# Transposing a retention head's normalised rows by DMA, as two planes of 16-bit halves, in place of TensorE

## The chip, the core and the metric

The kernel runs on one core of a Trainium2 chip. A core has five engines that each work through their own list of instructions in order: TensorE (PE, matmuls; its weight loads are PEld), VectorE (DVE), ScalarE (ACT), GpSimd (POOL) and SyncE (SP), which here issues all the DMAs. [...] On-chip data lie in SBUF, 128 partitions; a matmul writes into one of the banks of PSUM, which the other engines then read. DMAs move data between HBM and SBUF, and between places of SBUF. The metric is the device time of one execution in microseconds; lower is better.

## The reference

One layer of a hybrid decoder trunk on 2048 rows of width 1024, with 16 learned rows put ahead of them. What matters here, in the reference's words:

```python
hn = rms_norm(h, norm_g)
proj = jnp.einsum('bld,de->ble', hn, w_in)
cx, cb, cc, cg, q, k, v, rg = jnp.split(proj, N_PROJ, axis=-1)
conv_out = short_conv_branch(cx, cb, cc, conv_w) * jax.nn.silu(cg)
qf = rotary(q, pos) * d ** -0.5;  kf = rotary(k, pos)
ret = head_group_norm(retention_chunkwise(qf, kf, vf), ret_norm_g)
ret_out = ret.astype(h.dtype) * jax.nn.silu(rg)
mixed = jnp.concatenate([conv_out, ret_out], axis=-1)
h = h + jnp.einsum('ble,ed->bld', mixed, w_out)      # then a final rms_norm
```

There are four retention heads of 128 columns and four groups of 128 columns of the convolution. The retention of a head works on chunks of 128 rows. `head_group_norm` takes mean and variance over a head's 128 columns in each row, and the result is multiplied by a gain and by silu of the gate `rg`. The layer is in float32.

## The kernel before

**Stages.** The 2048 rows are worked in two stages of 1024 (`r` = 0, 1), each of two halves of 512 (`j` = 0, 1), and after them comes the output projection in eight pairs of row blocks. A stage has eight units: four convolution groups and four retention heads. Stage one runs group 0 first, then heads 0 to 3, then the other groups; stage two heads 0 to 3, then the groups (`UNITS`, line 36).

**A unit** has two quads. A quad (lines 203 to 238) makes a 2 by 2 arrangement of 128 by 512 blocks of the input projection by Strassen's scheme, in Winograd's form: seven products, each of 12 matmuls of 512 columns (four slices of the inner dimension, each as three matmuls on values split into a high part and a remainder). The products accumulate in three PSUM banks: xb, yb and zb. The tag of these banks, `pj`, has four, taken in rotation, so product 1 of a quad (its yb) goes into the bank that held yb of the quad before. ScalarE copies some of the banks out (`tc`, line 219) and VectorE adds (`take`). A bank can be written again once its `take` has read it: for the first quad of a head the `take` of yb is the addition that makes the first kv tile (line 587, at the helper's line 110).

**Weights.** `stationary` (line 123) takes four loaded blocks (`ra`, line 436 issues the loads), makes three combinations on GpSimd, and splits each of the seven into `wh` (ScalarE's cast, line 101) and `wl` (VectorE's subtraction, line 113), in rings of three.

**A head's tail.** After its second quad, the head (line 575) transposes k and v, makes the states, and for each half `j` the scores (`sc`, line 659), the masked scores (`pm`, line 661) and the output `o` (lines 669 and 670, eight short matmuls into one bank). Then it normalises: statistics on VectorE (lines 675 and 677), the root on GpSimd (`rp`, line 682), the normalised rows `y` on VectorE (line 686). Four transposes on TensorE (line 693) into a bank `yT` put rows and columns the way the gate lies, and VectorE multiplies by gain and gate (line 694); `store_mixed` sends the half out (line 444).

**What sets the order.** The program is written unit by unit, but a scheduler of the framework puts each engine's instructions into an order by its own estimate of their times; so a head's tail is worked in among the matmuls of the next unit's first quad. The order is fixed when the program is built. DMAs wait on SyncE in their order: a DMA that waits holds back those behind it.

**Beside the heads** a generator prepares the combinations of the next operand: after heads 1 and 2 of stage one, eight loads of x (line 361), four to each step, are scaled on ScalarE (line 177), combined on VectorE (`block_sums`, line 174 and line 113) and stored (line 190). After heads 1 and 2 of stage two the same is done with w_out, without the scaling. General tiles (`gen`, line 92) come from one pool of 16, taken in rotation: x, kv, q, the gates, and others.

Of the kernel before, what the change touches and what calls it, by code (L numbers as in the profile page):

```python
# [8 lines left out]
F32 = mybir.dt.float32  # L9
F32R = mybir.dt.float32r  # L10
BF16 = mybir.dt.bfloat16
AF = mybir.ActivationFunctionType
ALU = mybir.AluOpType

P = 128
# [6 lines left out]
HB = 512  # L22
# [48 lines left out]
def hybrid_trunk(ctx: ExitStack, tc: tile.TileContext, t, out: bass.AP, chunk_decay):  # L71
# [51 lines left out]
    def stationary(blocks):  # L123

        a11, a12, a21, a22 = blocks
        s1 = sb.tile([P, HB], F32, name="sa", tag="ra", bufs=RAW)

        def parts(src):
            hi = sb.tile([P, HB], F32R, name="wh", tag="wh", bufs=RING)
            lo = sb.tile([P, HB], F32R, name="wl", tag="wl", bufs=RING)  # L130
            split(hi, lo, src)
            return hi, lo

        w = [parts(a11), parts(a12)]
        add(nc.gpsimd, s1, a21, a22)
        sub(nc.gpsimd, a21, a11, a21)
        sub(nc.gpsimd, a11, s1, a11)
        sub(nc.gpsimd, a12, a12, a11)
        return w + [parts(a) for a in (a11, s1, a21, a12, a22)]
# [53 lines left out]
    def prepared(m, src, ns, held={}):  # L193

        for n in ns:
            for kt in range(KH):
# [3 lines left out]
                    nc.sync.dma_start(a, src[n, kt])  # L200
                parts(m, SUMS[n], kt, a)

    def quad(w, m, take):


        def product(i, bank, first):
            (wh, wl) = w[i]
            for kt in range(KH):
                ks = slice(kt * P, (kt + 1) * P)
                mh, ml = m[i][kt]  # L210
                for n, (a, b) in enumerate(((wl, mh), (wh, ml), (wh, mh))):
                    nc.tensor.matmul(  # L212
                        bank, a[:, ks], b, start=first and kt == 0 and n == 0, stop=kt == KH - 1 and n == 2,
                        skip_group_check=not first,
                    )

        def copy(bank):
            c = sb.tile([P, HB], F32, name="tc", tag="tc", bufs=COPIES)
            nc.scalar.copy(out=c, in_=bank)  # L219
            return c  # L220

        xb = ps_proj()
        product(0, xb, True)
        c = copy(xb)
        yb = ps_proj()
        product(1, yb, True)
        take(0, 0, yb, c)
        product(2, xb, False)
        u2 = copy(xb)
        zb = ps_proj()  # L230
        product(3, zb, True)
        c = copy(zb)
        product(4, xb, False)
        take(1, 1, xb, c)
        product(5, zb, False)
        take(0, 1, zb, u2)
        product(6, xb, False)
        take(1, 0, xb, None)
# [276 lines left out]
    def conv_group(g, r, m, f, blocks, ahead):  # L515
# [20 lines left out]

        blocks, meta = blocks
        quad(stationary(blocks), m, take)
        if meta:
            meta_carry(g, meta)  # L540
        carry(u, g, r)
# [24 lines left out]
    def rotary(a, table):  # L566
# [5 lines left out]
        nc.vector.tensor_tensor(out=a, in0=a, in1=table[:, 0, :], op=ALU.mult)  # L572
        turned[0] = nc.vector.tensor_tensor(out=a, in0=a, in1=rot[:, :w], op=ALU.add)

    def head(h, r, m, rot_t, f, blocks, ahead, first=(), between=()):


# [16 lines left out]
        if len(first) > 0:  # L594
            quad_plain(first[0], m, take)
        else:
            quad(stationary(blocks[0]), m, take)
        next(between, lambda: None)()
        q, sg = [None, None], [None, None]

# [54 lines left out]
        for j in range(2):  # L655
# [28 lines left out]
            for c in range(CH):  # L684
# [2 lines left out]
                    out=y[:, cs], in0=o[:, cs], scalar1=mv[:, c, 0:1], scalar2=rp[:, c, :],  # L687
                    op0=ALU.subtract, op1=ALU.mult,
                )
            yT = ps_misc()  # L690
            for c in range(CH):
                cs = slice(c * P, (c + 1) * P)
                nc.tensor.transpose(yT[:, cs], y[:, cs], ident)  # L693
            nc.vector.scalar_tensor_tensor(
                out=sg[j], in0=yT, scalar=ret_g[:, h : h + 1], in1=sg[j], op0=ALU.mult, op1=ALU.mult
            )
            store_mixed(r, j, KH + h, sg[j])
        if r < NR - 1:
            nc.gpsimd.tensor_copy(out=state[h], in_=states[-1])
        return blocks  # L700
# [203 lines left out]
```

## Time and profile before

| | |
|---|---|
| median of 3 runs | 894.16 us (893.94 to 894.59) |
| the profiled execution | 893.76 us |
| its span | 892.0 us |
| TensorE busy | 879.8 us, 99% of the span |
| VectorE busy | 717.7 us, 80% |
| ScalarE busy | 407.2 us, 46% |
| GpSimd busy | 397.8 us, 45% |
| moved by DMA | 116.94 MB, 131 GB/s on the mean |
| transposes of y on TensorE | 64, in 16 groups of four |

The span is the time from the first to the last record of the profile; the execution's own time is 1.8 us longer. In the profile a line such as L212 is line 212 of the kernel; the instructions of a helper (`add`, line 110; `sub`, line 113; the cast of `split`, line 101) all have the helper's line, so they are told apart by their tiles: `wl<-ra,wh` is a weight's remainder, `kv<-pj,tc` a kv tile taken from a bank. `128x512` is partitions by elements. What a matmul record shows as its duration (390 ns and more) overlaps the next; the distance between starts is its pace. In the changed kernel the lines are later by 3 (up to line 538), by 4 (to line 573) and then by 33 to 35, so L212 becomes L215, L669 and L670 become L704 and L705, and L686 becomes L721.

### The profile page before, as it was taken

Reading aid. Unit: us, or ns where it says so; the run is one execution under the profiler, and the core shown is the slowest. Engines: PE = TensorE matmul, PEld = TensorE weight load, DVE = VectorE, ACT = ScalarE, POOL = GpSimd, SP = SyncE. Lnnn points to the kernel's source line nnn. Section 1 sums busy time; section 2 is a strip of 40 time slices with the busy share of each in tenths; the row PEclk is TensorE's granted clock in tenths of the full one; section 3 lists DMA queues with packets and bytes.
Section 4 is the critical chain, followed back from the end, with each engine's and each line's share of the span. In section 5 each row is a group of like instructions: output and inputs, shape, how many; then the busy total and the mean of one; then the engine's idle time right before and its main releaser. Section 6 shows DMA issues by size and latency. Waiting matters only on the chain.

```text
span 892.0 us, 12867 instructions
## 1 busy us (share of the span) xinstructions
PE 879.8 (99%) x4407; PEld 725.0 (81%) x4407; DVE 717.7 (80%) x1176; ACT 407.2 (46%) x816; POOL 397.8 (45%) x291
## 2 busy tenths in 40 slices
PE   8999999999999999999999999999999999999996
PEld 5778788888888778888888888888888888788885
DVE  6788887988967966999889899777668699766764
ACT  8674424234245364746243332423333476545553
POOL 0554222313134654452323323345546454787773
PEclk9999999999999999999999999999999999999999
DMA  9711224354224252834135272313131393555532
GB/s 336 231 65 48 72 54 150 129 159 149 73 83 142 83 154 75 293 117 141 48 95 200 71 245 87 96 58 95 49 93 49 117 390 101 183 165 160 183 121 81
DMA packets 76242, 116.94 MB, mean 131 GB/s; under 512 B 7632, under 2 KB 24336, under 8 KB 76176
## 3 DMA queue, kind: packets, MB, share of 16 engines
q1 hardware_dynamic: 76176, 116.11, 40.3%
q8 instruction: 35, 0.57, 0.3%
q14 instruction: 31, 0.25, 0.1%
HBM read 90.92 MB, written 25.17 MB: 130 GB/s over the span
## 4 chain that ended last, share of the span: by engine, by line
PE 82%; DVE 8%; DMA 4%; issue 2%; ACT 2%; POOL 2%; SPq 0%; POOLq 0%; DVEq 0%; ACTq 0%
PE pj L212 66%; PE pj L262 6%; DVE ml L113 2%; PE ms L669 1%; PE ms L670 1%; PE ms L659 1%; PE ms L646 1%; DMA w<-in_w_out 1%; DMA ra<-in_w_in 1%; PE ms L397 1%; DVE wl L113 1%; PE ms L693 1%; DVE ml L105 1%; PE ms L631 1%; PE ms L636 1%
## 5 line engine op out<-in xcount | busy, mean ns | idle before, releaser
L212 PE MATMUL pj<-mh,wl 128*128 128x512 f32 x1008 | 399.1, 396 | 1.5 <-ACT wh L101 0.6
L212 PE MATMUL pj<-ml,wh 128*128 128x512 f32 x1008 | 393.3, 390 | 0.0
L212 PE MATMUL pj<-mh,wh 128*128 128x512 f32 x1008 | 393.0, 390 | 0.0
L101 ACT CAST wh<-ra 128x512 fp32r<-128x512 f32 x216 | 134.0, 621 | 311.0 <-PE pj L212 264.9
L212 PEld LDWEIGHTS pj<-mh,wl 128*128 128x128 f32 x1008 | 189.4, 188 | 43.2 <-issue 2.2
L113 DVE TENSOR_TENSOR wl<-ra,wh 128x512 fp32r<-128x512 f32 x216 | 194.1, 899 | 34.5 <-ACT wh L101 34.0
L212 PEld LDWEIGHTS pj<-mh,wh 128*128 128x128 f32 x1008 | 189.2, 188 | 39.9
L212 PEld LDWEIGHTS pj<-ml,wh 128*128 128x128 f32 x1008 | 189.5, 188 | 37.8 <-issue 0.5
L113 POOL TENSOR_TENSOR ra<-ra 128x512 f32<-128x512 f32 x72 | 112.8, 1566 | 84.1 <-DVE qg L614 32.3
L110 POOL TENSOR_TENSOR sa<-ra 128x512 f32<-128x512 f32 x36 | 54.9, 1526 | 120.6 <-DVE wl L113 53.1
L113 POOL TENSOR_TENSOR ra<-sa,ra 128x512 f32<-128x512 f32 x36 | 52.0, 1444 | 92.6 <-DVE wl L113 89.1
L219 ACT COPY tc<-pj 128x512 f32<-128x512 f32 x108 | 62.7, 580 | 0.0
L262 PE MATMUL pj<-ml,mh 128*128 128x512 f32 x128 | 50.2, 392 | 0.1
L262 PE MATMUL pj<-mh,mh 128*128 128x512 f32 x128 | 49.9, 392 | 0.0
L262 PE MATMUL pj<-mh,ml 128*128 128x512 f32 x128 | 48.7, 397 | 0.7 <-DVE ml L113 0.6
L682 POOL TENSOR_TENSOR rp<-rs,neg_half 128x4 f32<-128x4 f32 x16 | 19.9, 1246 | 48.1 <-DVE rs L110 47.8
L723 DVE TENSOR_TENSOR yo<-pj,yo 128x512 f32<-128x512 f32 x32 | 21.9, 686 | 17.6 <-PE pj L212 7.8
L101 ACT CAST wh<-sa 128x512 fp32r<-128x512 f32 x36 | 22.4, 621 | 29.1 <-PE pj L212 28.9
L522 POOL TENSOR_TENSOR c<-c,rr 128x512 f32<-128x512 f32 x14 | 26.1, 1865 | 19.6 <-DVE c L459 9.6
L686 DVE TENSOR_SCALAR pm<-ms,mv,rp 128x128 f32<-128x128 f32 x64 | 21.9, 404 | 15.8 <-POOL rp L682 15.8
L522 POOL TENSOR_TENSOR c<-c,tc 128x512 f32<-128x512 f32 x14 | 26.1, 1862 | 18.7 <-ACT tc L548 18.7
L728 POOL TENSOR_TENSOR z<-yo,final_g 128x512 f32<-128x512 f32 x16 | 26.9, 1682 | 15.9 <-DVE yo L723 15.9
(137 smaller groups left out, 1145.5 us busy)
## 6 DMA issues: line engine op xcount, KB each, us to landing
ra<-in_w_in SPq DMA_DIRECT2D x128, 256.0 KB, 2.7
x<-in_xT SPq DMA_DIRECT2D x48, 256.0 KB, 4.8
w<-in_w_out SPq DMA_DIRECT2D x32, 256.0 KB, 5.2
ra<-mixed SPq DMA_DIRECT2D x32, 256.0 KB, 2.6
yo<-in_x SPq DMA_DIRECT2D x32, 256.0 KB, 4.5
ra<-in_x SPq DMA_DIRECT2D x16, 256.0 KB, 3.2
mixed<-c SPq DMA_DIRECT2D x16, 256.0 KB, 2.6
mixed<-qg SPq DMA_DIRECT2D x16, 256.0 KB, 2.3
```

Source lines behind the costliest of these rows:

```text
L101: nc.scalar.copy(out=hi, in_=src)
L105: nc.vector.scalar_tensor_tensor(out=lo, in0=src, scalar=scale, in1=hi.bitcast(F32), op0=ALU.mult, op1=ALU.subtract)
L110: eng.tensor_tensor(out=out, in0=a, in1=b, op=ALU.add)
L113: eng.tensor_tensor(out=out, in0=a, in1=b, op=ALU.subtract)
L212: nc.tensor.matmul(bank, a[:, ks], b, start=first and kt == 0 and n == 0, stop=kt == KH - 1 and n == 2, skip_group_check=not first,)
L219: nc.scalar.copy(out=c, in_=bank)
L262: nc.tensor.matmul(banks[i], a[:, ks], b, start=half + kt + n == 0, stop=half == 1 and kt == KH - 1 and n == 2,)
L522: eng.tensor_tensor(out=out, in0=a, in1=b, op=ALU.mult)
L682: nc.gpsimd.tensor_tensor(out=rp, in0=rs, in1=neg_half.rearrange("p (c a) -> p c a", a=1), op=ALU.pow)
L686: nc.vector.tensor_scalar(out=y[:, cs], in0=o[:, cs], scalar1=mv[:, c, 0:1], scalar2=rp[:, c, :], op0=ALU.subtract, op1=ALU.mult,)
L723: last[0] = nc.vector.tensor_tensor(out=y, in0=pp, in1=y, op=ALU.add)
L728: nc.gpsimd.tensor_tensor(out=ys[i][j], in0=y, in1=final_g[:, j * HB : (j + 1) * HB], op=ALU.mult)
```

## The change

A head no longer transposes `y` on TensorE. ScalarE copies `y` into a tile `pl` so that the low 16 bits of all its 512 values stand in one plane and the high 16 bits in another. One DMA with transposing, issued by SyncE, takes `pl` as eight blocks of 128 by 128 16-bit values and writes the transposed blocks into a tile `tr`. A second copy of ScalarE puts the two planes together again, into a tile `wo`. VectorE's multiplication by gain and gate then reads `wo` in SBUF in place of a PSUM bank. The copy back, the gating and the store of both halves are put on a list (`pending`) and are written into the program only after the next unit's first quad (`catch_up`); an edge keeps ScalarE's part of them behind the quad's last copy out of a bank. The three new tiles come from the pool of 16 general tiles, whose size stays.

```diff
+    copied = [None]
...
-            nc.scalar.copy(out=c, in_=bank)
+            copied[0] = nc.scalar.copy(out=c, in_=bank)
...
         quad(stationary(blocks), m, take)
+        catch_up()
...
+    def halves(a):
+        return a.bitcast(U16).rearrange("p (n two) -> p two n", two=2)
+
+    def planes(a):
+        return a.bitcast(U16).rearrange("p (two n) -> p two n", two=2)
+
+    def turn(a):
+        apart, across = gen("pl")[:, :HB], gen("tr")[:, :HB]
+        nc.scalar.copy(out=planes(apart), in_=halves(a))
+        nc.sync.dma_start(
+            across.bitcast(U16).rearrange("p (c f) -> p c f", c=2 * CH), apart.bitcast(U16), transpose=True
+        )
+        return across
+
+    def whole(across):
+        a = gen("wo")[:, :HB]
+        nc.scalar.copy(out=halves(a), in_=planes(across))
+        return a
+
+    pending = []
+
+    def catch_up():
+        if pending:
+            with tc.issue_after(copied[0].ins):
+                while pending:
+                    pending.pop(0)()
...
             quad(stationary(blocks[0]), m, take)
+            catch_up()
...
-            yT = ps_misc()
-            for c in range(CH):
-                cs = slice(c * P, (c + 1) * P)
-                nc.tensor.transpose(yT[:, cs], y[:, cs], ident)
-            nc.vector.scalar_tensor_tensor(
-                out=sg[j], in0=yT, scalar=ret_g[:, h : h + 1], in1=sg[j], op0=ALU.mult, op1=ALU.mult
-            )
-            store_mixed(r, j, KH + h, sg[j])
+
+            def finish(j=j, across=turn(y)):
+                nc.vector.scalar_tensor_tensor(
+                    out=sg[j], in0=whole(across), scalar=ret_g[:, h : h + 1], in1=sg[j], op0=ALU.mult, op1=ALU.mult
+                )
+                store_mixed(r, j, KH + h, sg[j])
+
+            pending.append(finish)
```

The change moves instructions on every engine around a head's tail. Three places follow. Numbers behind a name tell buffers of one name apart, `x4` at a row's end is four equal rows.

**First place: VectorE in stage one, from head 0's tail to head 1.** Before, around the first half's normalisation (`st_1168` to `pm_1157`; `kv_1296`, the first kv tile of head 1, stands 16 rows further up):

```order
L113 TENSOR_TENSOR wl_1265<-ra_1070,wh_1264 128x512
L110 TENSOR_TENSOR kv_1344<-pj_1268,tc_1330 128x512
L113 TENSOR_TENSOR wl_1389<-ra_1379,wh_1388 128x512
L675 BN_STATS st_1168<-ms_1159 128x6 x4
L677 BN_AGGR mv_1169<-st_1168 128x2 x4
L110 TENSOR_TENSOR rs_1178<-mv_1169,ev_402 128x4
L686 TENSOR_SCALAR pm_1157<-ms_1159,mv_1169,rp_1180 128x128 x4
L110 TENSOR_TENSOR kv_1358<-pj_1317,tc_1315 128x512
```

Now, around the second half's normalisation (`st_1206` to `pm_1195`):

```order
L114 TENSOR_TENSOR wl_1403<-ra_1381,wh_1402 128x512
L710 BN_STATS st_1206<-ms_1197 128x6 x4
L712 BN_AGGR mv_1207<-st_1206 128x2 x4
L111 TENSOR_TENSOR rs_1216<-mv_1207,ev_442 128x4
L721 TENSOR_SCALAR pm_1195<-ms_1197,mv_1207,rp_1218 128x128 x4
L111 TENSOR_TENSOR kv_1290<-pj_1277,tc_1275 128x512
L111 TENSOR_TENSOR kv_1338<-pj_1262,tc_1324 128x512
L111 TENSOR_TENSOR kv_1352<-pj_1311,tc_1309 128x512
```

Before, two of the three additions that free banks (`kv_1296`, `kv_1344`) stood ahead of the head's normalisation; now all three stand behind the normalisation of both halves.

TensorE at this place now (`ms_1197` is the output of the second half, `pj_1422` product 0 of head 1's second quad and `pj_1437` its product 1, which takes the bank of `pj_1277`):

```order
L215 MATMUL pj_1422<-mh03_145,wh_1390 128x512
L704 MATMUL ms_1197<-kv_838,pm_1195 128x128
L705 MATMUL ms_1197<-state_1121,qg_1025 128x128
L704 MATMUL ms_1197<-kv_838,pm_1195 128x128
L705 MATMUL ms_1197<-state_1144,qg_1025 128x128
L704 MATMUL ms_1197<-kv_838,pm_1195 128x128
L705 MATMUL ms_1197<-state_1146,qg_1025 128x128
L704 MATMUL ms_1197<-kv_838,pm_1195 128x128
L705 MATMUL ms_1197<-state_1148,qg_1025 128x128
L215 MATMUL pj_1437<-mh10_163,wl_1395 128x512
```

Before, products 5 and 6 of the first quad and most of product 0 of the second stood behind the first half's eight short matmuls, and the second half's came one product later, behind product 1. Now product 1 follows the second half's directly.

**Second place: stage one, from head 1's tail to head 2** (and the same from 2 to 3). SyncE before (`mixed` are the stores of a finished half, `x` the loads and `sums_x` the stores of the preparation):

```order
L415 DMA mr<-in_rot_m 16x256
L436 DMA ra<-in_w_in 128x512
L444 DMA mixed_89<-qg 128x4x128
L361 DMA x<-in_xT 128x512 x8
L190 DMA sums_x<-x 128x512
L436 DMA ra<-in_w_in 128x512
L190 DMA sums_x<-x 128x512 x4
```

and now:

```order
L439 DMA ra<-in_w_in 128x512 x6
L590 DMA_TRANSPOSE tr<-pl 128x8x128
L439 DMA ra<-in_w_in 128x512
L590 DMA_TRANSPOSE tr<-pl 128x8x128
L364 DMA x<-in_xT 128x512 x8
L191 DMA sums_x<-x 128x512 x8
L447 DMA mixed_88<-qg 128x4x128
```

VectorE there now (`pm_1678` is the second half's normalised rows, `x_1714` a step of the preparation, `kv_1807` the first kv tile of head 2):

```order
L710 BN_STATS st_1689<-ms_1680 128x6 x4
L712 BN_AGGR mv_1690<-st_1689 128x2 x4
L111 TENSOR_TENSOR rs_1699<-mv_1690,ev_442 128x4
L721 TENSOR_SCALAR pm_1678<-ms_1680,mv_1690,rp_1701 128x128 x4
L175 SCALAR_TENSOR_TENSOR x_1714<-x_1714,gain_69,x_1712 128x512
L111 TENSOR_TENSOR kv_1807<-pj_1794,tc_1792 128x512
L111 TENSOR_TENSOR kv_1855<-pj_1779,tc_1841 128x512
```

The x loads stood behind the store of a finished half and now stand behind both transposing DMAs; a step that uses two of them now stands between the normalisation and the first kv addition. On TensorE the order there is that of the first place.

**Third place: stage two, from head 1's tail to head 2** (and from 2 to 3), VectorE now (`w_4877` and `w_4875` are two loads of w_out, issued behind both transposing DMAs):

```order
L710 BN_STATS st_4853<-ms_4844 128x6 x4
L712 BN_AGGR mv_4854<-st_4853 128x2 x4
L111 TENSOR_TENSOR rs_4863<-mv_4854,ev_3797 128x4
L721 TENSOR_SCALAR pm_4842<-ms_4844,mv_4854,rp_4865 128x128 x4
L114 TENSOR_TENSOR wl_5073<-ra_5061,wh_5072 128x512
L114 TENSOR_TENSOR wl_5081<-ra_5059,wh_5080 128x512
L114 TENSOR_TENSOR w_4877<-w_4877,w_4875 128x512
L111 TENSOR_TENSOR kv_4968<-pj_4955,tc_4953 128x512
```

Here too the first kv addition stands behind the second half's normalisation and behind a step of the preparation. On TensorE three products (the last of the old first quad but one, product 0 and product 2 of the next quad) stand between that half's short matmuls and product 1, which needs the bank.

More of the change, by code (lines that the diff above doesn't have):

```diff
@@ L11 @@
 BF16 = mybir.dt.bfloat16
+U16 = mybir.dt.uint16
 AF = mybir.ActivationFunctionType
```

## The prediction

> **What bounds the kernel now.** I read the page first, then the chain of waits, then TensorE's waits, then the timeline at the tail of a head. The page's busy shares, slices and chain:
>
> ```profile
> PE 879.8 (99%) x4407; PEld 725.0 (81%) x4407; DVE 717.7 (80%) x1176; ACT 407.2 (46%) x816; POOL 397.8 (45%) x291
> PE   8999999999999999999999999999999999999996
> PEclk9999999999999999999999999999999999999999
> PE 82%; DVE 8%; DMA 4%; issue 2%; ACT 2%; POOL 2%; SPq 0%; POOLq 0%; DVEq 0%; ACTq 0%
> ```
>
> TensorE is busy in every slice at the full granted clock, and 82% of the chain is its own. A busy TensorE need not be at its peak, so the pace counts. Two pieces of the chain in order of time (start, us, what), then three rows of TensorE's waits (us in total, times, longest):
>
> ```profile
> 118.63 7.50 PE pj L212 x33
> 767.63 117.31 PE pj L212 x516
> ...
> PE pj L212 <- ACT wh L101: 0.6, 1, 0.6
> PE pj L212 <- ACT tc L219: 0.5, 1, 0.5
> PE ms L693 <- DVE pm L686: 0.3, 1, 0.3
> ```
>
> Both pieces go at 0.227 us a 512-column matmul (7.50/33, 117.31/516), and hardly any matmul waits. So whatever leaves TensorE is won in full, and whatever makes it wait is lost in full. The order of its instructions is fixed, so a lost wait is not made up later.
>
> **What is removed: 64 transposes.** All of L693, and one group of four in the timeline (start, duration):
>
> ```profile
> L693 PEld LDWEIGHTS ms<-ident,pm x64: 138/140/146, 125.7 to 605.9; 128*128 128x128 f32 x64
> L693 PE MATMUL ms<-ident,pm x64: 270/272/329, 126.0 to 606.1; 128*128 128x128 f32 x64
> ...
> 140.48 0.39 PE L212 MATMUL pj<-mh,wh 128*128 128x512 f32 x1
> 140.72 0.60 PE L693 MATMUL ms<-ident,pm 128*128 128x128 f32 x4
> 141.07 0.48 PE L212 MATMUL pj<-mh,wl 128*128 128x512 f32 x1
> 141.38 0.40 PE L212 MATMUL pj<-ml,wh 128*128 128x512 f32 x1
> ```
>
> The 270 ns overlap. From 140.48 to 141.38 pass 0.90 us, in which two plain matmuls would take 0.45; the four transposes cost 0.45, handover included. 16 groups: **-7.1 us**. Below that only 6 us or so could be meant, where a group stands among other short matmuls; more than 7.1 is not there.
>
> **What hides.** 32 ScalarE copies of 1024 halves are added. A 512-column copy and the smallest instruction beside it:
>
> ```profile
> L101 ACT CAST wh<-ra 128x512 fp32r<-128x512 f32 x216 | 134.0, 621 | 311.0 <-PE pj L212 264.9
> L321 ACT ACTIVATION_READ_ACCUMULATOR n<-n x16: 185/187/192, 281.4 to 332.6; 128x1 f32 x16
> ```
>
> 0.62 for 512 and 0.19 for one element give about 1.06 us for 1024 (estimate; no less than 0.62, no more than 1.24). 34 us in all are covered by ScalarE's 311 us of idling ahead of these casts, 265 of it for TensorE; without that cover they would cost up to 34. The gating on VectorE keeps its count and reads SBUF in place of PSUM: nothing. 16 transfers of 256 KB are 4 MB beside 117: nothing by volume.
>
> **What is moved: a chain of VectorE now stands ahead of a bank that TensorE needs.** In the order of the changed kernel the last eight short matmuls of a head (its second half's output, L704 and L705) stand directly ahead of product 1 of the next quad. That product writes the bank of product 1 of the quad before, which VectorE frees with the addition of the first kv tile. Ahead of this addition VectorE now has the second half's whole normalisation, which needs those same short matmuls. So TensorE stands still from the end of them until statistics, square root, normalisation and addition are through. In the kernel before, 33 matmuls of 512 columns stood between the first half's output and the first matmul that needs anything behind its chain. The same chain, once, in the timeline of before (TensorE's first matmul behind the short ones, then VectorE, with GpSimd's root):
>
> ```profile
> 118.39 0.48 PE L212 MATMUL pj<-mh,wl 128*128 128x512 f32 x1
> ...
> 118.67 0.89 DVE L675 BATCH_NORM_STATS2 st<-ms 128x6 f32<-128x128 f32 x4 [0.43 <-PE ms L670]
> 119.48 0.36 DVE L677 BATCH_NORM_AGGREGATE mv<-st 128x2 f32<-128x6 f32 x4
> 119.87 0.17 DVE L110 TENSOR_TENSOR rs<-mv,ev 128x4 f32<-128x4 f32 x1
> 121.17 1.37 DVE L686 TENSOR_SCALAR pm<-ms,mv,rp 128x128 f32<-128x128 f32 x4 [1.13 <-POOL rp L682]
> 122.46 0.68 DVE L110 TENSOR_TENSOR kv<-pj,tc 128x512 f32<-128x512 f32 x1
> ...
> 120.12 1.02 POOL L682 TENSOR_TENSOR rp<-rs,neg_half 128x4 f32<-128x4 f32 x1
> ```
>
> Counted from 118.39, when TensorE could go on, normalisation ends at +4.15 and the addition at +4.75. **First stage, head 0 to head 1: +4.75 us.** Less only if the additions were ahead of the chain, which the order excludes.
>
> **First stage, heads 1 to 2 and 2 to 3: more.** There the order puts one step of preparing x (L175) between the chain and the addition. It needs x loads which SyncE issues only behind the second transposing DMA, and that DMA waits for ScalarE's copy of the normalised rows. The eight x loads of before, in a window of their own, and one such step of VectorE:
>
> ```profile
> L361 SPq DMA_DIRECT2D x<-in_xT x8: 382/400/457, 142.8 to 146.2; - x8
> ...
> DMA to landing us min/median/max: 3.0/4.0/4.7
> ...
> 154.44 0.74 DVE L174 SCALAR_TENSOR_TENSOR x<-x,gain 128x512 f32<-128x512 f32 x1
> ```
>
> From the same zero: 4.15 (normalised), +1.06 (copy into planes), + issue of the transposing DMA, + the second x load, + 0.74 + 0.68. The second load is issued 0.5 after the first and lands between 3.0 and 4.0 later, say 4.1 from the first issue. The issue is not in the trace: a plain one takes 0.40, eight of them (the instruction names eight blocks of 128 by 128) 3.2; I take 1.6, since it is one instruction with more to describe than a plain one, nearer to the lower row. Its 256 KB on the same queue delay the loads behind it: the first x load lands at 145.8 and the last at 150.9 (142.8 + 3.0, 146.2 + 4.7), seven gaps, 0.7 us each; I take 0.7 and as the upper end 5. Sum 13.0 us. Ends: 10.7 (copy 0.62, issue 0.40, no delay) and 18.8 (1.24, 3.2, 5). **Two places: +26.0.** In the kernel before nothing of the head waits for these x loads.
>
> **Second stage, heads 1 to 2 and 2 to 3.** The same with w_out in place of x (two loads, then a plain subtraction, 0.69 like the addition). But TensorE has three products, 36 matmuls or 8.2 us, between the short matmuls and the wait. 13.0 - 8.2 = 4.8, ends 2.4 and 10.6. **Two places: +9.6.** The other three tails of heads (each stage's last, and the second stage's first) have 24 to 36 matmuls, 5.4 to 8.2 us, ahead of the first wait on work behind the chain, against 4.15 + 0.7 for a low part or 4.75 + 0.7: nothing, at worst 1 each.
>
> **The clock after a stall.** Behind the last matmul (884.5) the granted clock stays full and is half from 889.5; and the first nine matmuls of all go at 0.40 (3.63/9). Two windows (length, then busy us of PE, PEld, DVE, ACT, POOL, PEclk) and the first group:
>
> ```profile
> 884.00:889.00 5.00, 0.92 (x5) 0.42 (x3) 2.54 (x6) 2.17 (x4) 1.10 (x2) 1.00 0.28 105
> 889.50:892.00 2.50, 0.00 (x0) 0.00 (x0) 0.00 (x0) 0.00 (x0) 0.00 (x0) 0.50 0.41 156
> ...
> 2.29 3.63 PE L766 MATMUL ms<-warm 128*128 128x512 bf16 x9 [2.29 <-ACT warm L760]
> ```
>
> So an idle time of over 4.5 us can halve the clock, and coming back costs about 9 x (0.40 - 0.227) = 1.6 us. I charge it to the four long stalls: **+6.4**; ends 0 and 8. [...]
>
> **Sum**, against the profiled execution's own 893.76 us (span 892.0 and 1.8 around it, 0.4 below the median of 894.16): -7.1 + 4.75 + 26.0 + 9.6 + 6.4 = +39.7, so **933 us**. With all lower ends -7.1 + 4.75 + 21.4 + 4.8 = +24, 918; with all upper ends -7.1 + 4.75 + 37.6 + 21.2 + 8 + 3 = +67, 961.
>
> **Rivals.**
> Only the removal counts (faster): 893.76 - 7.1 = 886.7 us. It takes that the first kv addition is through before TensorE's product 1, at the first three tails. For it speaks that today no matmul waits; against it the order, in which the addition stands behind the chain. It decides from the first tail on: a stall there under 2.4 us (7.1/3) at each of three would be needed to break even. Chance 0.05.
> The banks alone: the three tails of the first stage stall for 4.75 each, but x and w_out land early enough. 893.76 - 7.1 + 14.3 = 901 us. For it: loads in this trace usually come long before their use. Against it: they stand behind the second transposing DMA on SyncE, which needs the normalised rows. Chance 0.08.
> The transposing DMA is slow: its eight blocks go one after another. The smallest transfer of the trace that sits in this loop:
>
> ```profile
> mr<-in_rot_m SPq DMA_DIRECT2D x4, 16.0 KB, 2.4
> ```
>
> Eight times 2.4 is 19 us; midway to 0.7, 10 us. The four long stalls grow by 9.3 each, 37 in all, and in the other four tails ScalarE's copy back of the second half, in order ahead of the casts, waits some 7 us beyond the 13 that TensorE leaves it, 28 in all: 933 + 65 = 998 us. For it: no row shows what transposing costs a queue. Against: plain rows of 256 KB land in 3 to 5 us however they are cut. Chance 0.09. [...]
>
> **How the numbers follow.** The forecast as summed has 0.78. The range takes in its ends, 918 and 961, and the second rival at 901, and a little beyond the upper end for stalls that follow a stall: 900 to 968; what is left out is the first rival, the third, and some 0.05 of the forecast's own tails. What can be told from no change is 0.2%, 1.8 us. Faster comes from the first rival alone, 0.05; the cases between it and the second give 0.02 within 0.2%; slower 0.93.
>
> **What would show it.** Right: no transposes of y on TensorE; TensorE idle ahead of pj matmuls at L215, put down to the kv addition (L111), four times 5 to 14 us and once about 5; in these gaps VectorE waiting first for GpSimd's root and then, in four, for ScalarE's x or a w_out load; a second digit of PEclk below 9 there. Wrong: a gap at the first tail under 2 us (the bank reading fails), x loads landing before the chain ends (901), ScalarE's copies back waiting for the transposing DMA (the third rival), or gaps elsewhere, at conv groups or in the output stage, where I expect none.

## The result and the profile after

The changed kernel takes **941.53 us** (median of 4 runs, 938.42 to 944.01) against 894.36 us (4 runs of the kernel before, 893.94 to 894.59): a ratio of 1.0523, 95% interval 1.0500 to 1.0546. It is 47 us slower. The forecast was 933 us, with a range of 900 to 968. Its profiled execution took 942.61 us (span 940.8), 48.85 more than that of before.

Busy times, slices and chain on the page of the changed kernel:

```profile
PE 882.6 (94%) x4343; PEld 724.0 (77%) x4343; DVE 711.6 (76%) x1176; ACT 443.3 (47%) x848; POOL 396.5 (42%) x291
PE   8999989869589999999999889899999999999996
PEclk9999999979899999999999999999999999999999
PE 57%; DVE 9%; issue 2%; DMA 2%; ACT 1%; POOL 1%; SPq 1%; POOLq 0%; DVEq 0%; ACTq 0%
```

TensorE's slices have holes now, and its own part of the chain falls from 82% to 57%. What it waited for (us in total, times, longest):

```profile
PE pj L215 <- DVE kv L111: 30.8, 5, 11.7
PE pj L215 <- DVE wl L114: 11.6, 8, 2.2
```

Before, no wait of this kind was over 0.6 us. **The first place**, the tail of head 0, in the timeline:

```profile
127.63 0.39 PE L705 MATMUL ms<-state,qg 128*128 128x128 f32 x2
...
128.05 0.89 DVE L710 BATCH_NORM_STATS2 st<-ms 128x6 f32<-128x128 f32 x4 [0.39 <-PE ms L705]
...
130.54 1.37 DVE L721 TENSOR_SCALAR pm<-ms,mv,rp 128x128 f32<-128x128 f32 x4 [1.12 <-POOL rp L717]
131.82 1.87 DVE L111 TENSOR_TENSOR kv<-pj,tc 128x512 f32<-128x512 f32 x3
...
132.56 0.50 PE L215 MATMUL pj<-mh,wl 128*128 128x512 f32 x1 [4.54 <-DVE kv L111]
```

Between TensorE's last short matmul and the first kv addition stands the whole normalisation, and TensorE waits 4.54 us. **The second place**, the tail of head 1 (SPq is SyncE issuing DMAs):

```profile
186.02 1.36 DVE L721 TENSOR_SCALAR pm<-ms,mv,rp 128x128 f32<-128x128 f32 x4 [1.12 <-POOL rp L717]
187.42 1.04 ACT L589 COPY pl<-pm 128x1024 uint16<-128x1024 uint16 x1 [5.00 <-DVE pm L721]
188.49 1.24 SPq L590 DMA_TRANSPOSE tr<-pl  x1
189.78 3.90 SPq L364 DMA_DIRECT2D x<-in_xT  x8
192.88 0.72 ACT L178 ACTIVATE x<-x,gain 128x512 f32<-128x512 f32 x1 [4.42 <-DMA x<-in_xT]
193.64 0.75 DVE L175 SCALAR_TENSOR_TENSOR x<-x,gain 128x512 f32<-128x512 f32 x1 [6.25 <-ACT x L178]
194.30 1.28 DVE L111 TENSOR_TENSOR kv<-pj,tc 128x512 f32<-128x512 f32 x2
...
195.04 0.80 PE L215 MATMUL pj<-mh,wl 128*128 128x512 f32 x1 [11.55 <-DVE kv L111]
```

The chain is to be read row by row: normalised at 187.4, copied at 188.5, transposing DMA issued by 189.7, first x load landed at 192.9, scaled by 193.6, x step, addition, matmul. The same stall at the tail of head 2 is 11.69 us long.

**The third place**, heads 1 and 2 of stage two. TensorE's waits from 520 to 560 us (from 580 to 616 us they are the same three rows, with 3.5, 2, 1.9 in the first):

```profile
PE pj L215 <- DVE wl L114: 4.1, 3, 1.6
PE pj L215 <- DVE kv L111: 1.5, 1, 1.5
PE ms L681 <- ACT kv L675: 0.7, 1, 0.7
```

Here it is 6.3 and 5.7 us, in five and four short waits and not in one. At head 1 the first two, and between them the step of w_out on VectorE:

```profile
533.65 0.47 PE L215 MATMUL pj<-mh,wl 128*128 128x512 f32 x1 [1.58 <-DVE wl L114]
...
536.76 0.69 DVE L114 TENSOR_TENSOR w<-w 128x512 f32<-128x512 f32 x1 [3.26 <-DMA w<-in_w_out]
...
538.11 0.50 PE L215 MATMUL pj<-mh,wl 128*128 128x512 f32 x1 [1.49 <-DVE kv L111]
```

w_out lands late, as was expected: VectorE waits 3.26 us for it, ahead of the kv addition. But only the wait of 1.49 us stands behind that. The wait of 1.58 us, for a weight's remainder ahead of product 2, ends before the step begins. The other three come after product 1.

**The clock.** The windows of the changed kernel in which the granted clock was half (length, then busy us of PE, PEld, DVE, ACT and POOL with counts, PEclk, DMA share, GB/s):

```profile
133.32:136.73 3.41, 3.41 (x9) 2.65 (x8) 3.28 (x6) 0.15 (x1) 0.00 (x0) 0.50 0.34 77
187.93:198.17 10.24, 3.13 (x7) 2.51 (x8) 4.50 (x7) 2.56 (x4) 0.00 (x0) 0.50 0.82 237
252.78:263.02 10.24, 3.04 (x7) 2.46 (x8) 4.42 (x7) 2.51 (x4) 0.00 (x0) 0.50 0.82 265
607.77:614.60 6.83, 6.14 (x16) 4.89 (x16) 5.94 (x9) 0.62 (x2) 1.60 (x1) 0.50 0.46 150
```

In the second and third the drop falls largely into the stall. At 0.227 us each the matmuls of the first three are 2.0, 1.6 and 1.6 us of work: 1.4, 1.5 and 1.4 us are lost. The 16 of the fourth (two of them short) are 3.4 us: 2.7 us are lost.

**The sum.** Removal -7 (below), first place 4.5, second 11.55 + 11.69 = 23.2, third 12.0, clock 7.0, and short waits behind the stalls of stage one 5.8 (0.7 to 2.2 us each, for a remainder of a weight or an addition): 45.5 of the 48.85 us. The rest is spread in pieces of under one us.

### The profile page after: what moved, and what is told of

Read it like the earlier page. It is cut to its first block, busy times and chain, and to the rows that moved or that the text cites. A ratio compares the mean times of both kernels' runs of the same rounds, so it can differ in the third digit from the quotient of the medians.

```text
span 940.8 us, 12803 instructions
## 1 busy us (share of the span) xinstructions
PE 882.6 (94%) x4343; PEld 724.0 (77%) x4343; DVE 711.6 (76%) x1176; ACT 443.3 (47%) x848; POOL 396.5 (42%) x291
## 4 chain that ended last, share of the span: by engine, by line
PE 57%; DVE 9%; issue 2%; DMA 2%; ACT 1%; POOL 1%; SPq 1%; POOLq 0%; DVEq 0%; ACTq 0%
PE pj L215 50%; DVE ml L114 2%; PE pj L265 2%; DVE wl L114 1%; PE ms L705 1%; PE ms L694 1%; PE ms L704 1%; DMA w<-in_w_out 1%; PE ms L681 1%; DVE w L114 1%; DMA ra<-in_w_in 1%; DVE c L462 1%; DVE ml L106 1%; DVE qg L727 0%; DVE rot L574 0%
## 5 line engine op out<-in xcount | busy, mean ns | idle before, releaser
L717 POOL TENSOR_TENSOR rp<-rs,neg_half 128x4 f32<-128x4 f32 x16 | 16.7, 1041 | 46.3 <-DVE rs L111 46.0
```

Of the source, the lines that this page charges most:

```text
L717: nc.gpsimd.tensor_tensor(out=rp, in0=rs, in1=neg_half.rearrange("p (c a) -> p c a", a=1), op=ALU.pow)
```

## The experiments

Ten kernels were run. Two of them turn out, as built, to be the same program as another of the ten, so that eight are different. Each was timed beside the kernel before on the same chip, which took 894.05 us in the first four experiments, 894.85 in the next four and 894.74 in the last two. Two questions were open: what puts the kv additions behind the normalisation, and what the change is worth without that.

### The three new tiles off the pool of 16

By the program as built, the first kv tile of head 2 (stage one) lies in the buffer of head 1's second v tile, which the second half's output reads; the second in a q tile of that half; the third and fourth in head 1's two `pl` tiles. In the kernel before, all four lay in buffers of x tiles that had been stored. So the additions cannot come before that half's output any more. That suggested theory A: not the DMA but six tiles more per head, drawn from the rotation of 16, move the additions.

```diff
-    def turn(a):
+    def turn(a, apart, across):
-        apart, across = gen("pl")[:, :HB], gen("tr")[:, :HB]
...
-    def whole(across):
-        a = gen("wo")[:, :HB]
+    def whole(across, a):
...
-            def finish(j=j, across=turn(y)):
+            def finish(j=j, across=turn(y, k[j], q[j])):
-                    out=sg[j], in0=whole(across), scalar=ret_g[:, h : h + 1], in1=sg[j], op0=ALU.mult, op1=ALU.mult
+                    out=sg[j], in0=whole(across, vt[j]), scalar=ret_g[:, h : h + 1], in1=sg[j], op0=ALU.mult, op1=ALU.mult
```

> Everything the change does is kept (copies of 16-bit halves, transposing DMA, late gating); only the places of the three new tiles differ: pl, tr and wo go into the head's own k, q and v tiles, which are no longer read by then, so that the pool of 16 general tiles turns as in the kernel before (8 tiles a head, not 14). In this order the first kv additions stand ahead of the second half's normalisation again, and 37 matmuls of 512 columns stand between the first half's output and TensorE's first wait behind its chain. Theory A (the new tiles' places in the pool move the kv additions, and with them all the stalls): no stall at the head tails, 894.2 - 7.1 = 887 us, 885 to 890. Theory B (the longer way of the normalised rows itself, two copies, a transposing DMA and late gating, holds VectorE and then TensorE): 930 to 942 us, as the change.

Measured: **898.05 us**, ratio 1.0046 (1.0034 to 1.0059). The long stalls are gone: 43 of the 47 us were the tiles' places in the pool. But the 887 us of theory A were missed by 11. VectorE's order at head 0's tail shows the first part (`kv_1286` and `kv_1334` are the first two kv tiles of head 1, `st_1168` the first half's statistics, `st_1204` the second's):

```
L111 TENSOR_TENSOR kv_1286<-pj_1273,tc_1271 128x512
...
L111 TENSOR_TENSOR kv_1334<-pj_1258,tc_1320 128x512
L114 TENSOR_TENSOR wl_1385<-ra_1375,wh_1384 128x512
L708 BN_STATS st_1168<-ms_1159 128x6 x4
...
L708 BN_STATS st_1204<-ms_1195 128x6 x4
```

What is left is seen in TensorE's waits, then in ScalarE's (the copy back is now called `kv<-qg`, since it writes into the v tile):

```profile
PE pj L215 <- ACT tc L222: 5.2, 5, 1.5
```

```profile
ACT kv L595 <- DMA qg<-kv: 32.5, 15, 3.8
```

ScalarE waits 15 times for the transposing DMA, and since it works in order, the copies that empty TensorE's banks wait with it. One such place in the timeline:

```profile
189.10 1.34 ACT L595 COPY kv<-qg 128x1024 uint16<-128x1024 uint16 x1 [3.29 <-DMA qg<-kv]
...
190.82 0.58 ACT L222 COPY tc<-pj 128x512 f32<-128x512 f32 x1
...
191.45 0.50 PE L215 MATMUL pj<-mh,wl 128*128 128x512 f32 x1 [1.48 <-ACT tc L222]
```

That is a cost of the new path itself, of a kind that the prediction had put at nothing.

### The same with the gating at once

```diff
-            pending.append(finish)
+            finish()
```

> As the kernel with the dead tiles, but the copy back, the gating and the store are written at once, ahead of the next unit's quad, as before the change. Theory A: the order of the kv additions is that of the kernel before here too, and the gating waits for the DMA (3 us) off TensorE's path: 887 us, within 1 us of the kernel with the dead tiles. A third theory, C (the late gating is what keeps the DMA's time hidden): VectorE waits for some 5 us in each of 16 halves (copy 1.05, issue 1.24, landing 3.0 less the issue, copy back 1.37); with 8 us of cover by matmuls at half of them it would cost 5 us or more, 892 to 930 us.

Measured: 898.97 us, ratio 1.0051 (1.0039 to 1.0064), the same as with the late gating within the spread of the two (897.4 to 899.86 against 897.34 to 899.65). It could not be otherwise: both sources give the same program. Every engine has the same instructions in the same order, in the two traces as well. Writing the gating behind one quad or at once changes nothing, and theory C was not tested. What the pair shows is how far one program differs from itself: 0.9 us by the medians, and in the traces 5.2 against 7.4 us of TensorE's waits for ScalarE's copies. ScalarE's wait for the DMA is 32.5 us in both.

### The removal alone

The kernel before, its four transposes taken out.

```diff
-            yT = ps_misc()
-            for c in range(CH):
-                cs = slice(c * P, (c + 1) * P)
-                nc.tensor.transpose(yT[:, cs], y[:, cs], ident)
...
-                out=sg[j], in0=yT, scalar=ret_g[:, h : h + 1], in1=sg[j], op0=ALU.mult, op1=ALU.mult
+                out=sg[j], in0=y, scalar=ret_g[:, h : h + 1], in1=sg[j], op0=ALU.mult, op1=ALU.mult
```

> The kernel before without its 64 transposes of the normalised rows and with nothing in their place: the gate multiplies the rows as they lie, so the transposition is left out of the computation. It prices the removal alone. The sum of the prediction has 7.1 us for it: 894.2 - 7.1 = 887.1 us, 886 to 889. If the transposes had stood in TensorE's idle time, it would be 894; if their waits had cost TensorE more than their own 0.45 us a group, below 886. Against the kernel with the dead tiles: the same within 1 us, if the copies and the DMAs are hidden.

Measured: 889.88 us, ratio 0.9953 (0.9940 to 0.9967), 4.2 us faster and not 7.1. The order changes with the removal, and new small waits take part of it:

```profile
PE pj L212 <- ACT tc L219: 2.0, 2, 1.4
PE pj L212 <- DVE kv L110: 1.0, 2, 0.5
PE pj L262 <- ACT mh L104: 0.9, 1, 0.9
```

These three waits were 0.5, 0 and 0 before. Others became shorter; all of TensorE's waits together are 7.4 us in place of 4.7. So the 7.1 of work were there (4.2 + 2.7 = 6.9), and an order built anew need not pay them out in full.

### The pool alone

The opposite of the first experiment: the kernel before, its transposes on TensorE, with three more tiles from the pool in each half.

```diff
+            a = y
+            for name in ("pl", "tr", "wo"):
+                b = gen(name)
+                nc.scalar.copy(out=b[:, :1], in_=a[:, :1])
+                a = b
```

> The opposite experiment: the kernel before with all its transposes on TensorE and its gating at once, and in each half three tiles more from the pool of 16 (pl, tr, wo), each touched by a ScalarE copy of one column (0.19 us, 48 of them, 9 us on an engine that is 46% busy). No DMA, no planes, no late gating. In its order TensorE has one matmul between the second half's output and the product that waits for the first kv addition, as in the change, at three tails of stage one; behind heads 1 and 2 two steps of x and a gating stand between the normalisation and that addition. Theory A: a stall of about 4.7 us at the first of these and 5.5 to 8 at the other two, with about 1.5 us each for the clock, and in stage two 0 to 5 at each of two places: 894.2 + 20 to 35 = 914 to 929 us. Theory B: nothing but the tiny copies, 894 to 896 us.

Measured: **954.72 us**, ratio 1.0673 (1.0644 to 1.0703). With no DMA and no copy of more than one column the kernel loses 61 us, more than the change itself. Theory A had the sign and missed the size. TensorE's waits show what the expectation had left out:

```profile
PE pj L212 <- DVE kv L110: 17.3, 4, 5.8
PE ms L693 <- DVE pm L686: 12.7, 7, 3.0
```

In this order TensorE's own transposes of `y` also stand right behind the short matmuls, and wait for the normalisation (12.7 us) before the product waits for the addition (17.3). In the changed kernel that first wait is gone with the transposes. The clock takes a further part: its mean is 0.975 over the span of 950.5 us, and it is half for 44.4 us, in which TensorE is busy 29.8 us, so that about 15 us are lost by it (an estimate, half of 29.8). Together with the first experiment this settles the cause of the order: the same operations with the tiles elsewhere have no long stall, and the old operations with the tiles there stand still at the same tails, though by other amounts (5.9 us at heads 1 and 2 of stage one, 5.8 us at those of stage two).

### The steps of x and w_out behind the next quad

The changed kernel, with one call moved from the end of a head into the late list's place.

```diff
                 if unit > 0:
-                    next(later, None)
-                    next(later, None)
+                    prep[0] = later
...
                 while pending:
                     pending.pop(0)()
+            if prep[0]:
+                for _ in range(2):
+                    next(prep[0], None)
+                prep[0] = None
```

> The changed kernel, with one edit: the two steps that prepare x (in the second stage w_out) are written behind the next unit's first quad, not ahead of it. In the order no step of x stands between the second half's normalisation and the first kv addition any more; one matmul still stands ahead of TensorE's wait. The prediction's second place: its stall of 11.7 to 11.9 us is normalisation and addition (4.7, as at the first place) plus copy, transposing DMA, loads and a step of x. If so, both fall to 4.7 us: 941.5 - 14 = 927 us, and less, down to 915, as far as the short stalls behind them and those of the second stage (7 us at each of two heads) belong to the same steps. If the steps of x only filled time in which VectorE waited for something else, the stalls stay: 938 to 943.

Measured: 916.83 us, ratio 1.0249 (1.0236 to 1.0263), 24.7 us below the changed kernel. TensorE waits for kv additions three times, 4.5 us each. The second of the three in the timeline, behind head 1:

```profile
187.27 0.79 PE L215 MATMUL pj<-mh,wl 128*128 128x512 f32 x1 [4.54 <-DVE kv L111]
```

4.54 in place of 11.55 us, the very figure of the first place. In stage two TensorE waits 0.5 us at each of the two heads, in place of 6.3 and 5.7. So the additional part of the second place, and nearly all of the third, belong to the steps of x and w_out; the split that the prediction made is right.

### The transposing DMA on ScalarE's queue

```diff
-        nc.sync.dma_start(
+        nc.scalar.dma_start(
             across.bitcast(U16).rearrange("p (c f) -> p c f", c=2 * CH), apart.bitcast(U16), transpose=True
```

> The changed kernel, with one edit: the transposing DMA is issued by ScalarE and not by SyncE, so that the x and w_out loads no longer stand behind it on SyncE. The step of x stays ahead of the first kv addition. The prediction says that x is late because its loads stand behind the second transposing DMA: then each of the two long stalls of stage one falls to normalisation + step + addition, 4.15 + 0.74 + 0.68 = 5.6 us, 6.2 less each, and in the second stage up to 3 us at each of two heads: 941.5 - 12 to 18 = 923 to 930 us, with 1.24 us of issue more on ScalarE for each half. If x is late for another reason (the buffers that the x tiles take are freed late): 938 to 943.

Measured: 930.09 us, ratio 1.0399 (1.0386 to 1.0412), at the upper end of the range that was given, but not by the stalls that were given. The tail of head 1 in the timeline:

```profile
186.61 3.27 SPq L364 DMA_DIRECT2D x<-in_xT  x7
...
189.17 1.04 ACT L589 COPY pl<-pm 128x1024 uint16<-128x1024 uint16 x1 [5.02 <-DVE pm L721]
190.25 1.25 ACTq L590 DMA_TRANSPOSE tr<-pl  x1
191.54 0.72 ACT L178 ACTIVATE x<-x,gain 128x512 f32<-128x512 f32 x1 [1.33 <-issue]
192.30 0.75 DVE L175 SCALAR_TENSOR_TENSOR x<-x,gain 128x512 f32<-128x512 f32 x1 [3.16 <-ACT x L178]
192.97 1.88 DVE L111 TENSOR_TENSOR kv<-pj,tc 128x512 f32<-128x512 f32 x3
```

The x loads go out at 186.6, ahead of the normalisation, and are no longer what is late. But x is scaled on ScalarE, behind the copy into planes and now behind the issue as well, so TensorE's longest wait for the addition falls from 11.7 to 9.1 us and not to 5.6. The step of x was late for two reasons, one behind the other: its loads behind the DMA on SyncE, and its scaling behind the copy on ScalarE. The prediction named the first alone.

### The copy back on GpSimd

The kernel with the dead tiles, with one line changed.

```diff
-        nc.scalar.copy(out=halves(a), in_=planes(across))
+        nc.gpsimd.tensor_copy(out=halves(a), in_=planes(across))
```

> The kernel with the dead tiles, with one edit: the copy back that puts the two planes together goes to GpSimd, so that ScalarE no longer waits for the transposing DMA (it did 15 times, 32.5 us in all, with copies out of banks queued behind it). Theory D (that waiting in order on ScalarE is what the kernel with the dead tiles loses against the kernel that only leaves the transposes out, 898.05 - 889.88 = 8.2 us): most of the 8.2 comes back, 889 to 893 us. Theory E (the loss is the copies' own time on ScalarE, 1.04 + 1.36 us for each half): the copy into planes is 43% of it, so some 3.5 us stay, 893 to 895; or GpSimd, which waits in order as well and makes the weights' combinations, passes the wait on: 896 to 905.

Measured: 892.26 us, ratio 0.9979 (0.9971 to 0.9988): 5.8 of the 8.2 us come back (6 by the two ratios). That lies in theory D's range, but only 0.7 us from theory E's, so it does not decide alone; the next experiment does. GpSimd takes 1.51 us for a copy and waits for the DMA in ScalarE's stead (its group of instructions: busy us, mean ns, idle before it):

```profile
L595 POOL COPY kv<-qg 128x1024 uint16<-128x1024 uint16 x16 | 24.1, 1509 | 28.8 <-DMA qg<-kv 28.8
```

### The gating behind the second quad

The kernel with the dead tiles, ScalarE keeping both copies, with the late list worked off one quad later.

```diff
             quad(stationary(blocks[0]), m, take)
-            catch_up()
...
             quad(stationary(load_raw(w_loads(2 * h + 1))), m, take)
+        catch_up()
...
         quad(stationary(blocks), m, take)
-        catch_up()
...
         quad(stationary(load_raw(w_loads(n))), m, take)
+        catch_up()
```

> The kernel with the dead tiles, with one edit: the list of late gatings is worked off behind the next unit's second quad and not behind its first, so that the transposing DMA has landed when ScalarE comes to the copy back. ScalarE keeps both copies. Theory D: the waits for the DMA go, ScalarE's own 2.4 us for a half stay and fit between the copies out of banks: 889 to 893 us. Theory E: 896 to 899 us, no change from the kernel with the dead tiles.

Measured: **889.02 us** (886.97 to 891.80), ratio 0.9943 (0.9929 to 0.9957): faster than the kernel before by 5.8 us, and the fastest here that computes everything. The copy back by its shape, then what TensorE still waits for on ScalarE:

```profile
L595 ACT COPY kv<-qg 128x1024 uint16<-128x1024 uint16 x16 | 20.6, 1354 | 0.0
```

```profile
PE pj L215 <- ACT tc L222: 1.1, 1, 1.1
```

ScalarE does the same copies in the same time, and waits 0.0 us for the DMA where it waited 32.5. So theory D holds: not the copies' own 2.4 us for a half cost the 8 us, but the wait in front of others. The profiled execution, 886.97 us, is the fastest of its six; it is 6.8 below that of before (893.76).

### The last two: the later gating with GpSimd's copy, and the later gating without the dead tiles

The kernel with the gating behind the second quad, with the copy back on GpSimd (the one line above):

> The kernel with the gating behind the second quad (889.02 us), with one edit: the copy back goes to GpSimd (1.51 us each there, 16 times, on an engine that is 45% busy). If ScalarE's own 1.35 us for each half still cost something among its copies out of banks, it gets faster, by 1 to 2 us: 887 to 888 us. If nothing was left of it (ScalarE waited 0.0 us for the DMA there, and TensorE 1.1 us for one copy out of a bank), the same within 1 us, 888 to 890; if GpSimd's copies come ahead of the weights' combinations, slower, 890 to 893 us.

Measured: 893.05 us, ratio 0.9986 (0.9976 to 0.9996). This is not both cures together. The program built is that of the copy back on GpSimd (892.26 us), with the same instructions in the same order on every engine, so moving the list by a quad did nothing here, and GpSimd waited 28.5 us for the DMA as it had waited 28.8. Whether GpSimd's copy costs anything once its input is there was not tried.

The changed kernel, with the gating behind the second quad and the tiles from the pool:

> The changed kernel, with the late gatings worked off behind the next unit's second quad, and the three new tiles still from the pool of 16. It tells whether the tiles' places or the waits for the DMA carried the loss. Theory A (the places): the order still has one matmul between the second half's output and TensorE's wait at three tails of stage one, so the stalls of 4.7, 11.8 and 11.8 us stay: 935 to 942 us. Theory B (the waits for the DMA were the main thing): it falls by the 8 us that the waits cost in the kernel with the dead tiles or by more, 933 us or less.

Measured: 939.24 us, ratio 1.0499 (1.0483 to 1.0515). The stalls are the changed kernel's, and theory B falls:

```profile
PE pj L215 <- DVE kv L111: 33.4, 5, 11.7
```

## Why the prediction was right, and where it was off

**The removal, -7.1.** It was near the worth of the work: the best kernel is 5.8 us below that of before by the medians, and 6.8 by the profiled executions, of which its own was the fastest of six. The kernel that only removes got 4.2, and 2.7 more went into waits of its order. "More than 7.1 is not there" held.

**What hides.** This step failed as a statement on the new path, though it did not move the time of the changed kernel much. The two copies of the changed kernel as groups (busy us, mean ns, idle before them):

```profile
L597 ACT COPY wo<-tr 128x1024 uint16<-128x1024 uint16 x16 | 21.0, 1366 | 0.0
L589 ACT COPY pl<-pm 128x1024 uint16<-128x1024 uint16 x16 | 16.7, 1046 | 20.5 <-DVE pm L721 20.5
```

Both had been put at 1.06 us; the copy back takes 1.37. The step counted ScalarE's idle 311 us as cover and the DMA's time as nothing. It did not ask what ScalarE does while it waits for the DMA in order: 32.5 us of waiting with the bank copies behind it, worth 8.2 us in the kernel where the stalls don't hide it (898.05 against 889.88 us; 889.02 without the waits). In the changed kernel itself the long stalls gave the DMA time to land, and ScalarE waited 0.0 us for it. The volume was rightly put at nothing: the best kernel moves the same 121 MB. So was the gating: 744 ns each on the median, before out of PSUM and now out of SBUF.

**The first place, +4.75.** 4.54 us by the wait. The chain, the zero and the addition of terms were right to 0.2 us.

**The second place, +13.0 each.** 11.55 and 11.69 us. Mis-sized terms: the issue of the transposing DMA took 1.24 and not 1.6; no delay on the queue (0.7) is to be seen in the loads; and the second load was there 3.7 and 3.9 us after the first one's issue, not 4.1. At head 2 it decided, as the prediction has it: it landed at 258.5, behind the scaling (258.2) and just ahead of the step (258.58). At head 1 the first load (3.1 us after its issue) and ScalarE's scaling of it (0.72) ended 0.1 us later than the second load. The upper end of this term adds up to 19.1 and not 18.8, which takes the upper end of the whole sum from 961 to 962. The term that was missing, the scaling behind ScalarE's copy, is small while the loads are late, and it decides once they are not (the experiment with the other queue).

**The third place, +4.8 each.** 6.3 and 5.7 us of waits, above the value and inside the ends of 2.4 and 10.6, but in part by luck. The steps of w_out are the cause, since 0.5 us each is left when they are moved. The form was another. The stall at the kv addition, which the prediction prices, was 1.5 us at each head, below its lower end of 2.4, so of the four stalls of 5 to 14 us that were named as the sign, two did not come. With the wait for a weight's remainder ahead of product 2 TensorE waited 3.1 us up to product 1, in place of 4.8. The other 3.2 and 2.6 us are short waits behind product 1, which the sum did not have; by what way the steps of w_out make these is not shown.

**The clock, +6.4.** 7.0 us in all, near in sum by compensation: the 4.54 us stall also paid (1.4), the two long ones 1.5 and 1.4, the first head of stage two nothing and the second 2.7. The prediction had left the first place out, on a row that only bounded the limit at 4.5 us; the trace has half the clock behind its wait of 4.54 us, and the fourth window begins within a wait of 1.88 us, the longest there. The price of 1.6 us was luck in part: over the nine matmuls at 0.40 us from which it was taken (2.29 to 5.92 us) the profile gives a granted clock of 1.00.

**What the sum lacked.** Short waits behind the stalls of stage one, 5.8 us, were allowed for in the upper range and not in the sum. They, the third place (+2.4), the second (-2.8), the clock (+0.6) and some 3 us of small pieces make up most of what the time is above the forecast (8.5 us by the medians).

**The rivals.** The removal alone (886.7 us if the additions were through in time) is what the best kernel does, at 889.02; its condition, that the additions stand ahead, is what the tiles' places decide. The banks alone (901) needed x and w_out early; with their steps moved away it came to 916.83, with the stalls of 4.54 that it had named, and waits of 1.3 to 1.7 us behind them that it had not. The slow transposing DMA is refuted by the row of its sixteen issues and their landing:

```profile
L590 SPq DMA_TRANSPOSE tr<-pl x16: 1232/1239/1358, 125.5 to 643.6; - x16
...
DMA to landing us min/median/max: 2.7/3.0/3.2
```

3.0 us for eight blocks, like a plain load of its size (3.0 to 4.7 us for the eight x loads of before; the groups of 256 KB transfers there have medians of 2.0 to 5.2 us). The rival's 10 us for blocks one after another were an estimate, and the row does not bear it out.

**What the prediction took as given.** It read the order off and priced it, and never asked what had moved it. The cause, six tiles more in a rotation of 16, is shown by the two experiments on the tiles. Behind heads 1 and 2 the way from the tiles to the order can be named: the next kv tiles lie in buffers that the tail still reads. At the first place, behind head 0, the new buffers belong to the convolution group and are free early; why the scheduler puts the additions late there too stays open.

## What to carry to other kernels

A tile added to a rotating pool is not free even if it fits (43 of the 47 us here): it changes whose buffer the next user gets, and with a scheduler behind it the order of everything; put new short-lived tiles into buffers of the same unit that are dead by then, and look at who inherits which buffer. An engine's idle time covers an added copy only if the copy's input is there when its turn comes: an in-order wait for a DMA costs whatever is queued behind it (8.2 us here, for 32.5 us of waiting), so put the wait where the DMA has long landed. A stall is priced well by adding the rows of the chain (4.75 against 4.54 us at the first place), but every engine on the chain has its own queue: write down what stands ahead of each link on each engine. And an edit of the source need not change the program: two of the ten here did not.

## What the hardware showed that was not expected

In the trace of the changed kernel, up to its last matmul, the granted clock is half for 3.41, 10.24, 10.24 and 6.83 us: one, three, three and two pieces of 3.41 us. They lie on one grid: the four drops begin at 133.32, 187.93, 252.78 and 607.77 us, and the distances of 54.61, 64.85 and 354.99 us are 16, 19 and 104 times 3.413. Where a wait lay in the grid counted as well as its length. The kernel with the other queue has two waits of 2.38 us, from 527.51 and from 579.34 us. The piece in which each begins, and the next (length, busy us of TensorE, PEclk, DMA share, GB/s):

```profile
526.43:529.84 3.41, 1.08 (x5) 1.00 0.76 133
529.84:533.25 3.41, 3.36 (x8) 0.50 0.73 229
577.62:581.03 3.41, 1.72 (x8) 1.00 0.76 133
581.03:584.45 3.42, 2.73 (x12) 1.00 0.53 112
```

The first wait leaves TensorE idle for 2.33 us of one piece, and the next piece is at half the clock. The second is split over two pieces (1.69 and 0.68 us), and the clock stays. Waits of 1.9 us did both: in the two executions of the program with the dead tiles (gating late, and at once) a piece with 1.88 us of idling was followed by half the clock, and one with 1.79 us was not. In the changed kernel 1.87 us in the piece ahead of 607.77 were enough, and 1.89 us in the piece from 126.49 were not. In the traces of the kernel before and of the changed kernel, behind the first 10 us, no piece at full clock with less than 1.87 us of idling was followed by half, and every one with more than 1.89 us was. The pieces named here of the other kernels agree. This is read off the executions that there are; no run was made to vary it.

In the changed kernel, taking 512 values apart into halves took ScalarE 1.046 us, and putting them together 1.366 us, for the same 1024 halves. GpSimd took 1.51 us for the latter in the kernel with the copy back there.
